# Chunk attention by blocks: small matmuls in place of masked full products

## The chip, the cores and the metric

The kernel runs on one NeuronCore of one Trainium2 chip. The metric is the device time of one execution in microseconds; the time before is the median of three runs. Engines are named as in the profile: PE is the matmul engine (PEld its weight loads), DVE is VectorE, ACT is ScalarE, POOL is GpSimd, SP is SyncE, which issues most transfers.

## The reference

One layer of an encoder, applied with the same weights to a sequence of 256 tokens and one of 512 (768 rows together, 1024 wide, all fp32): three mixers side by side, an output projection, and an MLP of width 4096. The change is in the first mixer, gated linear attention (GLA) in both directions, with 4 heads of 64 key and 128 value channels:

```python
def gla_scan(q, k, v, logg):
    ...
    def step(state, inp):
        qi, ki, vi, gi = inp
        b = jnp.cumsum(gi, axis=1)
        diff = b[:, :, None] - b[:, None, :]
        decay = jnp.exp(jnp.where(mask[:, :, None, None], diff, -jnp.inf))
        attn = jnp.einsum('bihd,bjhd,bijhd->bijh', qi, ki, decay)
        o = (jnp.einsum('bijh,bjhe->bihe', attn, vi)
             + jnp.einsum('bihd,bhde->bihe', qi * jnp.exp(b), state))
    ...
    logg_f = (jax.nn.log_sigmoid((r_f @ wg_f + bg_f).astype(jnp.float32)) / GLA_GATE_NORM
    ...
    o = gla_scan(q, k, v, logg_f) + flip(gla_scan(flip(q), flip(k), flip(v), flip(logg_b)))
    o = rmsnorm(o.astype(gv.dtype), norm_g)
    o = o * jax.nn.silu(gg.reshape(b_, s, GLA_HEADS, GLA_DV))
```

The decay is one for each key channel, so the attention within a chunk is not one product of q and k with a matrix over it. The other two mixers (differential attention, and a state-space mixer `ssd` whose `ssd_dt` is touched too) and the MLP follow the usual formulas.

## The kernel before

All 768 rows are kept as 6 tiles of 128 tokens (`NT`, two of the first sequence, four of the second). Large products split each fp32 operand in a rounded high part and a rest and add three products (`mm3`, lines 97 to 99); weights come in units over SP's queue (`load_unit`), are split by ACT (line 133) and DVE (line 134), and are consumed by `tm_unit` (tokens on the output partitions) or `fm_unit` (features on them).

The GLA mixer works on chunks of 128 tokens and on head pairs: the 64 key channels of two heads lie on 128 partitions, tokens on the free axis. There are two head pairs, one after the other. `gla_gates` makes the prefix sums of the log gates within each chunk, `Pf` forward and `Pb` backward, by a scan on DVE, in a layout of 129 columns for each chunk, column 0 being zero, so that both the inclusive sum (columns 1 to 128) and the exclusive one (0 to 127) can be read. `gla_core` then makes the chunk states `S` and the scaled queries `qst`, and the attention within each chunk by a binary splitting of the 128 tokens. At level s (64, 32, 16, 8, 4, 2, 1) tokens of the left half of each block of 2s meet those of the right half; the decay is taken relative to the boundary between the halves, so it splits in a factor for the query and one for the key. For each level DVE forms four differences of half the columns (lines 417, 418, 423, 424), ACT takes the exponentials (419, 425), DVE multiplies by q (420) and POOL by k (426). Then PE multiplies the whole 128x128 product for each chunk and head (435), and DVE copies from it into the attention tile `A`, by a mask, the elements that belong to this level (436). The diagonal is made apart: q times k summed over channels by PE (394, the tile `dps`, copied to `dg`), applied when the output `gout` is read (451). Lines 446 and 447 make the output, from `A` and from the states.

No order is written out by hand: the tile framework has a scheduler that fixes each engine's order from estimates of its own, and the engines then run in that order, waiting on semaphores. So the projections of other parts of the kernel (`tm`, `fm`) stand between the attention levels on PE where the scheduler put them. Scratch buffers come from pools of fixed numbers (`t3`, `c4`, `s3`, `t2`), and the results of small PE work from five banks of PSUM (`mx`).

Of the kernel before, what the change touches and what calls it, by code (L numbers as in the profile page):

```python
# [19 lines left out]
P = 128  # L20
# [7 lines left out]
N_IN, N_S3, N_T3, N_T2, N_TT, N_CC, N_DL, N_RAW, N_ACC = 12, 6, 6, 4, 8, 5, 7, 2, 3  # L28
# [3 lines left out]
W129 = NT * 129  # L32
# [10 lines left out]
def hybrid_kernel(ctx, tc, io):  # L43
# [31 lines left out]
    s3 = tag(first, "s3", N_S3, 776)  # L75

# [15 lines left out]
    def bc(ap, shape):  # L92
        return ap.to_broadcast(shape)
# [153 lines left out]
    resetm = s3("resetm", n=W129)  # L247
    pool.memset(resetm, 1.0)
    pool.memset(resetm.rearrange("p (c w) -> p c w", w=129)[:, :, 0:1], 0.0)

    def v129(t):
        return t.rearrange("p (c w) -> p c w", w=129)
# [11 lines left out]
    def gla_gates(hp):  # L264
        c0 = hp * P
        pre = []
        for d, r in ((0, R_BF), (1, R_BB)):
            bias = col(r + hp)
            rngs = ((0, 512), (512, 256))
            zs = [mx("gate"), mx("gate")]  # L270
            t1, g = t3("gt1"), t3("gt2", n=W129)
            v2 = v129(g)
            pool.memset(v2[:, :, 0:1], 0.0)
# [7 lines left out]
            dve.tensor_tensor(v2[:, :, 1:129], v2[:, :, 1:129], v128(t1), ALU.subtract)  # L281
            pf = s3("pre", n=W129)
            prefix(pf, g)
            pre.append(v129(pf))
        return pre
# [40 lines left out]

    def gla_core(pre, qk, v):
        Pf, Pb = pre
# [4 lines left out]
        kst = [t3("kst") for _ in range(2)]  # L333
        ef, eb = t3("ef"), t3("eb")
        act.activation(v128(ef), Pf[:, :, 1:129], AF.Exp, scale=0.0625)
        dve.tensor_tensor(v128(eb), bc(Pb[:, :, 128:129], [P, NT, P]), Pb[:, :, 0:128], ALU.subtract)
# [8 lines left out]
        dve.tensor_tensor(v128(kf), bc(Pf[:, :, 128:129], [P, NT, P]), Pf[:, :, 1:129], ALU.subtract)  # L345
        act.activation(kf, kf, AF.Exp, scale=0.0625)
        act.activation(v128(kb), Pb[:, :, 0:128], AF.Exp, scale=0.0625)
# [39 lines left out]
        A = [c4("A", n=T) for _ in range(2)]  # L387
        for a in A:
            pool.memset(a, 0.0)
        prod = t3("prod")  # L390
        pool.tensor_tensor(prod, q, k, ALU.mult)
        dps = mx("dps")
        for c in range(NT):
            mm(dps[:, 2 * c:2 * c + 2], lhsT=prod[:, c * P:(c + 1) * P], rhs=sel2, start=True, stop=True)
        dg = small("dg", 12).rearrange("p (c h) -> p c h", h=2)
        act.copy(dg, dps[:, :12].rearrange("p (c h) -> p c h", h=2))
        for li, s in enumerate(LEVELS):
            nb = P // (2 * s)

            def halves(ap, right):  # L400
                if nb == 1:
                    return ap[:, :, right * s:right * s + s]
                return ap.rearrange("p c (b r s) -> p c b r s", b=nb, r=2)[:, :, :, right, :]

            def inc(pp, right):
                return halves(pp[:, :, 1:129], right)

            def exc(pp, right):
                return halves(pp[:, :, 0:128], right)

            def ref(pp):
                if nb == 1:
                    return bc(pp[:, :, s:s + 1], [P, NT, s])
                return bc(exc(pp, 1)[:, :, :, 0:1], [P, NT, nb, s])

            eq = t3("eq")
            dve.tensor_tensor(halves(v128(eq), 1), inc(Pf, 1), ref(Pf), ALU.subtract)
            dve.tensor_tensor(halves(v128(eq), 0), ref(Pb), exc(Pb, 0), ALU.subtract)
            act.activation(eq, eq, AF.Exp, scale=0.0625)
            dve.tensor_tensor(eq, eq, q, ALU.mult)  # L420
            if s > 1:
                ek = t3("ek")
                dve.tensor_tensor(halves(v128(ek), 0), ref(Pf), inc(Pf, 0), ALU.subtract)
                dve.tensor_tensor(halves(v128(ek), 1), exc(Pb, 1), ref(Pb), ALU.subtract)
                act.activation(ek, ek, AF.Exp, scale=0.0625)
                pool.tensor_tensor(ek, ek, k, ALU.mult)
            else:
                ek = k
            for (a, b) in ((0, 4), (4, 6)):
                for h in range(2):  # L430
                    hs = slice(64 * h, 64 * h + 64)
                    ps = mx("att")
                    for c in range(a, b):
                        cs = slice(c * P, (c + 1) * P)
                        mm(ps[:, (c - a) * P:(c - a + 1) * P], lhsT=ek[hs, cs], rhs=eq[hs, cs], start=True, stop=True)
                    dve.copy_predicated(v128(A[h])[:, a:b, :], bc(masks[:, li, None, :], [P, b - a, P]),
                                        v128(ps[:, :(b - a) * P]))
# [3 lines left out]
        for h in range(2):  # L441
            for (a, b) in ((0, 4), (4, 6)):
                ps = mx("gout")
                for c in range(a, b):
                    o = (c - a) * P
                    mm(ps[:, o:o + P], lhsT=v128(A[h])[:, c, :], rhs=v128(v[h])[:, c, :], start=True, stop=False)
                    mm(ps[:, o:o + P], lhsT=qst[h][:, c * P:(c + 1) * P], rhs=S[h][:, c, :], start=False, stop=True)
                for c in range(a, b):
                    o = (c - a) * P
                    ov = v128(o_sb[h])[:, c, :]  # L450
                    dve.scalar_tensor_tensor(ov, v128(v[h])[:, c, :], dg[:, c, h:h + 1], ps[:, o:o + P],
                                             op0=ALU.mult, op1=ALU.add)
                    act.activation(junk[:, :P], ov, AF.Square, accum_out=ss[:, h, c:c + 1])
# [23 lines left out]
    def ssd_dt():  # L477
# [14 lines left out]
        dtl = t3("dtl", n=W129)  # L492
        lv_ = v129(dtl[ps_])
        pool.memset(lv_[:, :, 0:1], 0.0)

        dve.tensor_scalar(lv_[:, :, 1:129], v128(stk[0:16]), sdtc[0:16, 3:4], -128.0, op0=ALU.mult, op1=ALU.max)
        pre = t3("dpre", n=W129)
        pr = v129(pre)[ps_]
        dve.tensor_tensor_scan(pre[ps_], resetm[ps_], dtl[ps_], 0.0, ALU.mult, ALU.add)
        act.copy(v128(stk[32:48]), pr[:, :, 1:129])  # L500
        act.copy(v128(stk[64:80]), pr[:, :, 0:128])
        tot = bc(pr[:, :, 128:129], [16, NT, P])
        dve.tensor_tensor(v128(stk[96:112]), tot, pr[:, :, 1:129], ALU.subtract)
        stb = t3("stb")
        dve.tensor_tensor(v128(stb[0:16]), tot, pr[:, :, 0:128], ALU.subtract)
# [3 lines left out]
        nc.sync.dma_start(out=scr[0:8, :].rearrange("h (c i) -> h c i", i=P), in_=pr[0:8, :, 1:129])  # L509
        nc.sync.dma_start(out=scr[8:16, :].rearrange("h (c i) -> h c i", i=P), in_=pr[8:16, :, 0:128])  # L510
        nc.sync.dma_start(out=scp, in_=pr[:, :, 128])
# [485 lines left out]
    def col(r):  # L997
        return cols[:, r:r + 1]

    half = const.tile([P, 42], F32, name="half")  # L1000
# [10 lines left out]
    masks = t2("masks").bitcast(U8)[:, :len(LEVELS) * P].rearrange("p (l i) -> p l i", i=P)  # L1011
    for a, b in ((0, 4), (4, 7)):
        mraw = t2("mraw", n=(b - a) * P).rearrange("p (l i) -> p l i", i=P)
        nc.sync.dma_start(out=mraw, in_=io["c_masks"][:, a:b, :])
        pool.tensor_copy(masks[:, a:b], mraw)
# [4 lines left out]
    sel2 = const.tile([P, 2], F32, name="sel2")  # L1020
    pool.memset(sel2, 0.0)
    pool.memset(sel2[0:64, 0:1], 2.0)
    pool.memset(sel2[64:128, 1:2], 2.0)
# [145 lines left out]
def _constants():  # L1169
    i = np.arange(P)  # L1170
    masks = np.zeros((P, len(LEVELS), P), np.float32)
    for n, s in enumerate(LEVELS):
        masks[:, n, :] = (i[:, None] // (2 * s) == i[None, :] // (2 * s)) & (i[:, None] // s != i[None, :] // s)
# [28 lines left out]
```

## Time and profile before

| what | value |
|---|---|
| time, median of 3 runs | 1186.19 us (1180.62 to 1189.1) |
| the profiled execution | 1190.88 us, span 1188.8 us, mean granted clock 0.978 |
| PE busy | 1136.2 us (96%) |
| PE weight loads | 999.4 us (84%) |
| DVE busy | 768.7 us (65%) |
| ACT busy | 541.1 us (46%) |
| POOL busy | 162.8 us (14%) |
| first and last attention matmul of the levels (L435) | 120.1 and 237.8 us |

Busy is the time in which an engine had at least one instruction in work. PE's matmuls overlap (one starts before the last ends), so PE's busy time says that there was work, not how fast it went; the starts of neighbouring matmuls say that. "Idle before" is the time in which the engine had nothing in work just ahead of instructions of a group, with what ended it. The granted clock is PE's; 1.00 is full speed.

### The profile page before, as it was taken

To read this page: it belongs to the slowest core of one execution; us is meant where nothing else is said; L and a number is where in the kernel's file an instruction comes from. 1 tells how busy PE (TensorE), PEld (TensorE's weight loads), DVE (VectorE), ACT (ScalarE), POOL (GpSimd) and SP (SyncE) were. 2 spreads that over 40 slices of the span, in tenths; PEclk is the share of its full clock that TensorE was granted. 3 is DMA by queue.
4 is the path that set the end of the run, shared out by engine and by line. 5 is a ranking of instruction groups with operands and counts; after the bars stand their busy time and mean duration, and the time that the engine had idled before them with its cause. 6 is when DMAs were issued, how large, how long until landed. Compare 5 with 4: busy or idle time off the path is not lost.

```text
span 1188.8 us, 17623 instructions
## 1 busy us (share of the span) xinstructions
PE 1136.2 (96%) x6788; PEld 999.4 (84%) x6788; DVE 768.7 (65%) x1366; ACT 541.1 (46%) x1037; POOL 162.8 (14%) x207
## 2 busy tenths in 40 slices
PE   7979999999999998899988999999999999999998
PEld 7979899899998887698878897787987788787786
DVE  6558979775479577896786687766544444444443
ACT  7455345256266426665765673435322322322331
POOL 2003324140310262110100002200000000000000
PEclk9989999799999999899999999999999999999999
DMA  6312021143254346245645457642232232232331
GB/s 193 96 39 69 4 63 37 36 155 119 65 172 113 109 149 203 74 142 185 186 131 171 134 164 236 228 150 72 72 106 92 86 106 87 91 107 79 99 106 71
DMA packets 118856, 136.62 MB, mean 115 GB/s; under 512 B 8951, under 2 KB 86901, under 8 KB 118773
## 3 DMA queue, kind: packets, MB, share of 16 engines
q1 hardware_dynamic: 118741, 135.50, 36.7%
q8 instruction: 53, 0.87, 0.3%
q14 instruction: 30, 0.25, 0.1%
q10 hardware_dynamic: 32, 0.01, 0.0%
HBM read 121.80 MB, written 13.68 MB: 114 GB/s over the span
## 4 chain that ended last, share of the span: by engine, by line
PE 41%; DMA 12%; DVE 9%; ACT 6%; issue 2%; POOL 0%; SPq 0%; ACTq 0%; DVEq 0%; POOLq 0%
DMA wr<-in_w_mlp 8%; PE tp L97 7%; PE tp L98 7%; PE tp L99 7%; PE fm L97 5%; PE fm L98 5%; PE fm L99 5%; DVE wl L134 3%; ACT wh L133 3%; DMA wr<-in_w_out 2%; DMA er<-scr 1%; DVE zh L558 1%; DVE xres L877 1%; PE tm L97 1%; PE tm L99 1%
## 5 line engine op out<-in xcount | busy, mean ns | idle before, releaser
L133 ACT CAST wh<-wr 128x1024 fp32r<-128x1024 f32 x186 | 189.2, 1048 | 250.5 <-PE tp L99 128.2
L134 DVE TENSOR_TENSOR wl<-wr,wh 128x1024 fp32r<-128x1024 f32 x186 | 228.8, 1252 | 107.7 <-ACT wh L133 105.8
L99 PE MATMUL tm<-wh,hTl 128*128 128x256 f32 x576 | 169.8, 295 | 0.0
L97 PE MATMUL tm<-wh,hTh 128*128 128x256 f32 x576 | 168.0, 292 | 1.7 <-ACT xp L552 1.6
L98 PE MATMUL tm<-wl,hTh 128*128 128x256 f32 x576 | 168.2, 292 | 0.0
L877 DVE TENSOR_TENSOR xres<-tp,xres 128x512 f32<-128x512 f32 x116 | 77.7, 686 | 98.3 <-PE tp L99 98.0
L97 PEld LDWEIGHTS tm<-wh,hTh 128*128 128x128 f32 x576 | 112.3, 195 | 4.0 <-ACT xp L552 1.8
L98 PEld LDWEIGHTS tm<-wl,hTh 128*128 128x128 f32 x576 | 112.1, 195 | 1.7 <-DVE wl L134 0.2
L99 PEld LDWEIGHTS tm<-wh,hTl 128*128 128x128 f32 x576 | 112.2, 195 | 1.3
L98 PE MATMUL fm<-h2l,wh 128*128 128x512 f32 (+1 forms) x288 | 107.1, 373 | 0.0
L97 PE MATMUL fm<-h2h,wh 128*128 128x512 f32 (+1 forms) x288 | 106.9, 373 | 0.0
L99 PE MATMUL fm<-h2h,wl 128*128 128x512 f32 (+1 forms) x288 | 106.7, 371 | 0.0
L97 PE MATMUL tp<-wh,uh 128*128 128x512 f32 x256 | 101.5, 396 | 0.6
L98 PE MATMUL tp<-wl,uh 128*128 128x512 f32 x256 | 100.5, 392 | 0.0
L99 PE MATMUL tp<-wh,ul 128*128 128x512 f32 x256 | 99.7, 395 | 0.0
L97 PE MATMUL fm<-h,wh 128*128 128x256 f32 x256 | 72.3, 284 | 2.4 <-ACT relu L923 2.1
L98 PE MATMUL fm<-h,wh 128*128 128x256 f32 x256 | 72.2, 283 | 0.0
L99 PE MATMUL fm<-h,wl 128*128 128x256 f32 x256 | 71.5, 283 | 0.6 <-DVE wl L134 0.6
L923 ACT ACTIVATE relu<-fm 128x256 f32<-128x256 f32 (+1 forms) x68 | 31.6, 468 | 70.3 <-PE fm L99 70.3
L97 PEld LDWEIGHTS fm<-h2h,wh 128*128 128x128 f32 x288 | 54.7, 190 | 10.1
L99 PEld LDWEIGHTS fm<-h2h,wl 128*128 128x128 f32 x288 | 54.6, 190 | 10.0
L98 PEld LDWEIGHTS fm<-h2l,wh 128*128 128x128 f32 x288 | 54.7, 190 | 9.9
(323 smaller groups left out, 2499.4 us busy)
## 6 DMA issues: line engine op xcount, KB each, us to landing
wr<-in_w_mlp SPq DMA_DIRECT2D x128, 512.0 KB
wr<-in_w_in SPq DMA_DIRECT2D x30, 512.0 KB
wr<-in_w_out SPq DMA_DIRECT2D x24, 512.0 KB
ar<-scr SPq DMA_DIRECT2D x6, 512.0 KB
er<-scr SPq DMA_DIRECT2D x6, 512.0 KB
x<-in_x_sample SPq DMA_DIRECT2D x4, 512.0 KB
wr<-in_w_in SPq DMA_DIRECT2D x8, 256.0 KB
xres<-in_x_sample SPq DMA_DIRECT2D x4, 512.0 KB
```

What stands on the lines that cost most here:

```text
L97: mm(out, lhsT=lh, rhs=rh, start=first, stop=False)
L98: mm(out, lhsT=lh, rhs=rl, start=False, stop=False)
L99: mm(out, lhsT=ll, rhs=rh, start=False, stop=last)
L133: act.copy(hi, raw)
L134: dve.tensor_tensor(lo, raw, rd(hi), ALU.subtract)
L558: dve.scalar_tensor_tensor(zh, xp[:, k:k + 772], half[:, 6 * k + j:6 * k + j + 1], zh, op0=ALU.mult, op1=ALU.add)
L877: dve.tensor_tensor(xres[t][:, cs], ps, xres[t][:, cs], ALU.add)
L923: act.activation(r, ps, AF.Relu)
```

## The change

The attention of each level is no longer made as whole 128x128 products.

- At level 64 PE makes only the two 64x64 blocks off the diagonal for each chunk and head, at level 32 the four 32x32 blocks beside the diagonal, and ACT copies them to their places in `A`. No mask is used.
- At the levels 16 to 1 PE makes the four 32x32 blocks on the diagonal for each chunk and head, and DVE copies by a mask, of 32 columns, into a small tile `L` (two heads x 6 chunks x 32 columns). The diagonal is one more such product (of 2q and k) with its own mask. At the end ACT copies `L` into the diagonal blocks of `A`. The matmuls write to output partitions that start at 0, 32, 64 or 96 (0 or 64 for the large blocks). The tiles `dps`, `dg` and `prod` go, and the output is copied from PSUM by ACT in place of DVE's multiply and add.
- The prefix sums lie in 128 columns for each chunk. They are kept with the other sign, `Xf` inclusive, `Xb` exclusive with a separate total `tot`; for that the gates take `Relu` on ACT in place of add and min on DVE.
- The differences of a level are made whole: one DVE operation over all 768 columns for each direction, into a tile `d` of 2 x 768, in place of two of half the columns each. The exponentials and products are then made of halves: two of 384 columns for each one of 768.
- `ssd_dt` uses the 128-wide layout too, with one more DVE operation (`exc`), and the pool `t3` has 4 buffers in place of 6.

```diff
@@ gla_gates
             for z, (o, n) in zip(zs, rngs):
                 act.activation(t1[:, o:o + n], z[:, :n], AF.Abs, bias=bias)
-                dve.tensor_scalar(v2[:, o // P:(o + n) // P, 1:129], v128(z[:, :n]), bias, 0.0, op0=ALU.add, op1=ALU.min)
+                act.activation(g[:, o:o + n], z[:, :n], AF.Relu, bias=nbias, scale=-1.0)
...
@@ gla_core
+    def into_local(L, ps, i):
+
+        dve.copy_predicated(L, bc(masks[:, i, None, :], [P, NT, 32]), ps)
...
-        A = [c4("A", n=T) for _ in range(2)]
-        for a in A:
-            pool.memset(a, 0.0)
-        prod = t3("prod")
-        pool.tensor_tensor(prod, q, k, ALU.mult)
-        dps = mx("dps")
-        for c in range(NT):
-            mm(dps[:, 2 * c:2 * c + 2], lhsT=prod[:, c * P:(c + 1) * P], rhs=sel2, start=True, stop=True)
...
+        A = [v128(c4("A", n=T)) for _ in range(2)]
+        L = t2("L", n=12 * 32).rearrange("p (h c i) -> p h c i", h=2, c=NT)
+        pool.memset(L, 0.0)
+        k3 = v128(k)
+
+        def blocks(ps, h, w, left, right, across):
+
+            hs = slice(64 * h, 64 * h + 64)
+            for c in range(NT):
+                for b in range(P // w):
+                    o = b ^ across
+                    mm(ps[w * b:w * b + w, c, :], lhsT=left[hs, c, w * b:w * b + w], rhs=right[hs, c, w * o:w * o + w],
+                       start=True, stop=True)
+
         for li, s in enumerate(LEVELS):
...
-            dve.tensor_tensor(halves(v128(eq), 1), inc(Pf, 1), ref(Pf), ALU.subtract)
-            dve.tensor_tensor(halves(v128(eq), 0), ref(Pb), exc(Pb, 0), ALU.subtract)
-            act.activation(eq, eq, AF.Exp, scale=0.0625)
-            dve.tensor_tensor(eq, eq, q, ALU.mult)
+            for i, X in enumerate((Xb, Xf)):
+                x = parts(X)
+                ref = x[:, :, 1, 0:1] if i == 0 else x[:, :, 0, s - 1:s]
+                dve.tensor_tensor(D[i].rearrange("p b r i -> p b (r i)"), X.rearrange("p (b i) -> p b i", i=2 * s),
+                                  bc(ref, [P, nb, 2 * s]), ALU.subtract)
+            eq = t3("eq")
+            for i in range(2):
+                act.activation(D[i][:, :, i], D[i][:, :, i], AF.Exp, scale=-0.0625)
+                dve.tensor_tensor(parts(eq)[:, :, i], D[i][:, :, i], parts(q)[:, :, i], ALU.mult)
...
-            for (a, b) in ((0, 4), (4, 6)):
+            left, right = v128(ek), v128(eq)
+            if s == 64:
                 for h in range(2):
-                    hs = slice(64 * h, 64 * h + 64)
-                    ps = mx("att")
-                    for c in range(a, b):
-                        cs = slice(c * P, (c + 1) * P)
-                        mm(ps[:, (c - a) * P:(c - a + 1) * P], lhsT=ek[hs, cs], rhs=eq[hs, cs], start=True, stop=True)
-                    dve.copy_predicated(v128(A[h])[:, a:b, :], bc(masks[:, li, None, :], [P, b - a, P]),
-                                        v128(ps[:, :(b - a) * P]))
+                    ps = mx("att")[:, :NT * 64].rearrange("p (c i) -> p c i", c=NT)
+                    blocks(ps, h, 64, left, right, 1)
+                    act.copy(A[h][0:64, :, 64:128], ps[0:64])
+                    act.copy(A[h][64:128, :, 0:64], ps[64:128])
+                continue
+            for h in range(2):
+                ps = mx("att")[:, :NT * 32].rearrange("p (c i) -> p c i", c=NT)
+                blocks(ps, h, 32, left, right, int(s == 32))
+                if s < 32:
+                    into_local(L[:, h], ps, LOCAL.index(s))
+                    continue
+                for b in range(4):
+                    o = 32 * (b ^ 1)
+                    act.copy(A[h][32 * b:32 * b + 32, :, o:o + 32], ps[32 * b:32 * b + 32])
+
+        q2 = t3("q2")
+        act.activation(q2, q, AF.Copy, scale=2.0)
+        for h in range(2):
+            ps = mx("att")[:, :NT * 32].rearrange("p (c i) -> p c i", c=NT)
+            blocks(ps, h, 32, k3, v128(q2), 0)
+            into_local(L[:, h], ps, LOCAL.index(0))
+            for b in range(4):
+                act.copy(A[h][32 * b:32 * b + 32, :, 32 * b:32 * b + 32], L[32 * b:32 * b + 32, h])
...
-                    dve.scalar_tensor_tensor(ov, v128(v[h])[:, c, :], dg[:, c, h:h + 1], ps[:, o:o + P],
-                                             op0=ALU.mult, op1=ALU.add)
+                act.copy(o_sb[h][:, a * P:b * P], ps[:, :(b - a) * P])
```

How the order of instructions changes is seen best on PE, in the levels of the first head pair. Here `att` is the PSUM tile of a level's product for one head (numbers tell tiles apart), `tm` a projection between. Before, at the levels 16 and 8:

```order
L97 MATMUL tm_1653<-wh_1590,hTh_134 128x256
L435 MATMUL att_1117<-eq_1101,ek_1106 128x128 x4
L435 MATMUL att_1123<-eq_1101,ek_1106 128x128 x2
L98 MATMUL tm_1653<-wl_1591,hTh_134 128x256
L99 MATMUL tm_1653<-wh_1590,hTl_135 128x256
L97 MATMUL tm_1706<-wh_1590,hTh_120 128x256
L98 MATMUL tm_1706<-wl_1591,hTh_120 128x256
L435 MATMUL att_1127<-eq_1101,ek_1106 128x128 x2
L435 MATMUL att_1141<-eq_1131,ek_1136 128x128 x4
L99 MATMUL tm_1706<-wh_1590,hTl_121 128x256
```

After, at the end of the levels (level 2, level 1, and the diagonal from `q2`):

```order
L99 MATMUL tm_1981<-wl_1866,hTh_129 128x256
L412 MATMUL att_1355<-eq_1345,ek_1350 32x32 x24
L412 MATMUL att_1381<-eq_1345,ek_1350 32x32 x24
L412 MATMUL att_1415<-eq_1410,gk_821 32x32 x24
L412 MATMUL att_1441<-eq_1410,gk_821 32x32 x24
L412 MATMUL att_1469<-q_204_1467,gk_821 32x32 x24
L412 MATMUL att_1499<-q_204_1467,gk_821 32x32 x24
L100 MATMUL tm_1981<-wh_1865,hTl_130 128x256
```

The attention stands in fewer and longer runs: 26 runs of 2 to 16 matmuls before, 12 runs of 1 to 144 after, with projections between. Of the 425 matmuls from the first to the last of the first head pair's levels 360 are attention after the change, of 192 before 84.

On DVE, at the same stage. Before (`eq` and `ek` are the query and key factors of a level, `A` the attention tile, `pre` the prefix sums, `S` the states, `gg` the output gate):

```order
L436 COPY_PREDICATED A_1027<-masks_777,att_1067 128x256
L417 TENSOR_TENSOR eq_1131<-pre_727 128x48x8
L381 SCALAR_TENSOR_TENSOR S_1005<-S_1005,dec_935,U_1013 64x128
L418 TENSOR_TENSOR eq_1131<-pre_743 128x48x8
L423 TENSOR_TENSOR ek_1136<-pre_727 128x48x8
L424 TENSOR_TENSOR ek_1136<-pre_743 128x48x8
L436 COPY_PREDICATED A_1026<-masks_777,att_1081 128x512
```

After (`d` is a whole difference, `L` the small tile):

```order
L428 TENSOR_TENSOR d_1407<-pre_731 128x768
L338 COPY_PREDICATED L_1031<-masks_787,att_1251 128x192
L433 TENSOR_TENSOR eq_1345<-d_1342,gq_820 128x192x2 x2
L330 SCALAR_TENSOR_TENSOR gg_1864<-gg_1864,tm_1928 128x256
L338 COPY_PREDICATED L_1031<-masks_787,att_1290 128x192
L338 COPY_PREDICATED L_1031<-masks_787,att_1316 128x192
L433 TENSOR_TENSOR eq_1410<-d_1407,gq_820 128x384 x2
L428 TENSOR_TENSOR d_2167<-pre_780 128x768
L428 TENSOR_TENSOR d_2167<-pre_765 128x768
```

Two differences for a level stand where there were four, the masked copies are shorter, and the differences of the second head pair (`d_2167`) follow before the first one's levels are done.

More of the change, by code (lines that the diff above doesn't have):

```diff
@@ L75, in hybrid_kernel @@
     s3 = tag(first, "s3", N_S3, 776)
+    d2 = tag(first, "d2", 2, 2 * T)
     def small(name, n):
@@ new lines, in gla_core, with parts @@
+        for li, s in enumerate(LEVELS):
+            nb = T // (2 * s)
+            d = d2("d")
+            def parts(t):
+                return t.rearrange("p (b r i) -> p b r i", r=2, i=s)
+            D = [parts(d[:, i * T:(i + 1) * T]) for i in range(2)]
+            for i, X in enumerate((Xb, Xf)):
[3 more added lines that the diff above has]
+                                  bc(ref, [P, nb, 2 * s]), ALU.subtract)
@@ L421, in gla_core @@
             if s > 1:
                 ek = t3("ek")
[L423 to L426, printed above, removed]
+                for i in range(2):
+                    act.activation(D[1 - i][:, :, i], D[1 - i][:, :, i], AF.Exp, scale=0.0625)
+                    pool.tensor_tensor(parts(ek)[:, :, i], D[1 - i][:, :, i], parts(k)[:, :, i], ALU.mult)
@@ L491, in ssd_dt @@
         dve.scalar_tensor_tensor(stk[0:16], z, 0.0, l, op0=ALU.max, op1=ALU.add)
[L492 to L503, printed above, removed]
+        dtl = t3("dtl")[ps_]
+        dve.tensor_scalar(dtl, stk[0:16], sdtc[0:16, 3:4], -128.0, op0=ALU.mult, op1=ALU.max)
+        inc, exc = t3("dpre")[ps_], t3("dexc")[ps_]
+        dve.tensor_tensor_scan(inc, resetm[ps_], dtl, 0.0, ALU.mult, ALU.add)
+        dve.tensor_tensor(exc, inc, dtl, ALU.subtract)
+        act.copy(stk[32:48], inc)
+        act.copy(stk[64:80], exc)
+        tot = bc(v128(inc)[:, :, 127:128], [16, NT, P])
+        dve.tensor_tensor(v128(stk[96:112]), tot, v128(inc), ALU.subtract)
         stb = t3("stb")
-        dve.tensor_tensor(v128(stb[0:16]), tot, pr[:, :, 0:128], ALU.subtract)
+        dve.tensor_tensor(v128(stb[0:16]), tot, v128(exc), ALU.subtract)
         scr = dram.tile([16, T], F32, name="scr")
         scp = dram.tile([16, NT], F32, name="scp")
-        nc.sync.dma_start(out=scr[0:8, :].rearrange("h (c i) -> h c i", i=P), in_=pr[0:8, :, 1:129])
-        nc.sync.dma_start(out=scr[8:16, :].rearrange("h (c i) -> h c i", i=P), in_=pr[8:16, :, 0:128])
-        nc.sync.dma_start(out=scp, in_=pr[:, :, 128])
+        nc.sync.dma_start(out=scr[0:8, :], in_=inc[0:8])
+        nc.sync.dma_start(out=scr[8:16, :], in_=exc[8:16])
+        nc.sync.dma_start(out=scp, in_=v128(inc)[:, :, 127])
         ptb = const.tile([P, 2, 8, NT], F32, name="ptb")
@@ L998, in col @@
         return cols[:, r:r + 1]
+    nbf = const.tile([P, 4], F32, name="nbf")
+    dve.tensor_scalar(nbf, cols[:, R_BF:R_BF + 4], -1.0, None, op0=ALU.mult)
     half = const.tile([P, 42], F32, name="half")
@@ L1009, in hybrid_kernel @@
     pre = [gla_gates(hp) for hp in range(2)]
[L1011 to L1015, printed above, removed]
+    masks = t2("masks").bitcast(U8)[:, :len(LOCAL) * 32].rearrange("p (l i) -> p l i", i=32)
+    mraw = t2("mraw", n=len(LOCAL) * 32).rearrange("p (l i) -> p l i", i=32)
+    nc.sync.dma_start(out=mraw, in_=io["c_masks"])
+    pool.tensor_copy(masks, mraw)
     tri = const.tile([P, 2, P], F32, name="tri")
@@ L1019, in hybrid_kernel @@
     nc.sync.dma_start(out=rope, in_=io["c_rope"])
[L1020 to L1023, printed above, removed]
     qk16 = small("qk16", 32).rearrange("p (a d) -> p a d", a=2)
```

74 lines of the change are left out of this document (32 added, 42 removed).

## The prediction

> **What bounds the kernel now.** First the page's busy times and its row of slices, which say whether an engine is full and when.
>
> ```profile
> PE 1136.2 (96%) x6788; PEld 999.4 (84%) x6788; DVE 768.7 (65%) x1366; ACT 541.1 (46%) x1037; POOL 162.8 (14%) x207
> PE   7979999999999998899988999999999999999998
> DVE  6558979775479577896786687766544444444443
> PEclk9989999799999999899999999999999999999999
> ```
>
> TensorE (PE) is full nearly all the time and VectorE (DVE) is not, except where the change is made: digits 5 to 9, that is 120 to 270 us. The windows there are next; after the times come PE, weight loads, DVE, ACT and POOL busy, each with its count, then the granted clock.
>
> ```profile
> core 0: us, PE busy (x) PEld busy (x) DVE busy (x) ACT busy (x) POOL busy (x), PEclk, DMA share, GB/s
> 120.00:150.00 30.00, 28.37 (x228) 25.26 (x227) 29.75 (x51) 10.33 (x15) 9.30 (x5) 0.94 0.00 1
> 150.00:180.00 30.00, 30.00 (x256) 29.24 (x256) 22.50 (x50) 13.85 (x40) 7.71 (x15) 1.00 0.20 62
> 180.00:210.00 30.00, 27.96 (x241) 26.58 (x241) 27.69 (x42) 16.02 (x30) 13.32 (x6) 1.00 0.12 36
> 210.00:240.00 30.00, 30.00 (x186) 27.07 (x186) 22.23 (x37) 5.44 (x7) 4.25 (x2) 0.72 0.13 36
> ```
>
> In the first of these DVE has 29.75 of 30 us, so the attention levels go at DVE's pace; but PE is at 28.37, because the scheduler put projection matmuls (`tm`) between the levels. In the second PE has no hole at all, weight loads fill 29.24 us, and 256 matmuls run; the last window has only 186, at clock 0.72. The answer: in this stage PE is the resource that ends last, DVE is close behind, and an edit counts mainly by the PE time that it takes.
>
> **The attention matmuls, removed and added.** The rows by shape (line, engine, operation, tile, count, total us, mean ns, then idle before):
>
> ```profile
> L435 PE MATMUL att<-eq,ek 64*128 64x128 f32 x288 | 36.0, 301 | 3.7 <-DVE A L436 2.4 <-DVE S L381 1.3
> L435 PE MATMUL att<-eq,gk 64*128 64x128 f32 x48 | 5.3, 287 | 0.0
> 60.00:250.00 190.00, 40.57 (x336) 34.79 (x336) 29.66 (x56) 0.92 0.15 44
> L394 PE MATMUL dps<-sel,prod 128*128 128x2 f32 x24 | 2.8, 244 | 0.0
> L531 PE MATMUL tmb<-ident,stb 16*128 16x16 f32 x6 | 0.5, 211 | 0.0
> L629 PE MATMUL U<-wx,btm 128*64 128x256 f32 x32 | 4.1, 389 | 0.0
> ```
>
> The third row is the window of the `att` tiles alone, with overlaps counted once; the last two give the length of other small matmuls, for use below. The program writes 7 levels x 2 heads x 6 chunks x 2 head pairs = 168 matmuls; the trace has 336, so each fp32 matmul is two instructions, each with its weight load. I call such an instruction with its load a pair. Removed: 40.6 us of `att` and 2.8 us of `dps`, 43.4 us.
>
> Added: per head pair 24 blocks of 64x64, and 48 blocks of 32x32 for each of the six lower levels and for the diagonal (336): 360 matmuls. For both head pairs 720, hence 1440 pairs, over four times as many, each with a quarter of the columns or half. All hangs on the price of a small pair. Five places of the trace bear on it:
>
> ```profile
> 156.88 0.39 PE L446 MATMUL gout<-gv,A 128*128 128x128 f32 x2
> 162.01 0.39 PE L447 MATMUL gout<-S,qst 128*128 128x128 f32 x2
> 113.15 1.29 PE L394 MATMUL dps<-sel,prod 128*128 128x2 f32 x11
> 64.52 0.54 PE L531 MATMUL tmb<-ident,stb 16*128 16x16 f32 x6
> 416.68 1.08 PE L629 MATMUL U<-wx,btm 128*64 128x256 f32 x8
> 145.27 0.38 PE L98 MATMUL tm<-wl,hTh 128*128 128x256 f32 x1
> 145.59 0.72 PE L435 MATMUL att<-eq,ek 64*128 64x128 f32 x8
> 146.24 0.39 PE L99 MATMUL tm<-wh,hTl 128*128 128x256 f32 x1
> 146.46 0.28 PE L97 MATMUL tm<-wh,hTh 128*128 128x256 f32 x1
> 146.58 0.28 PE L98 MATMUL tm<-wl,hTh 128*128 128x256 f32 x1
> ```
>
> The output products: 46 pairs lie between the starts 156.88 and 162.01, so 0.112 us a pair with 128 columns. The `dps` pairs have 2 columns: (1.29 - 0.24) / 10 = 0.105 us (the last one's own length taken off, from the rows above, here and in what follows). Fewer moving columns alone bought nothing. The small transposes `tmb`: (0.54 - 0.21) / 5 = 0.066 us. Then overlap: `U` writes two halves of the output partitions in turn with 64 weight columns each, and takes (1.08 - 0.39) / 7 = 0.099 us a pair of 256 columns, half of what two streams of 128 columns would take: two parts of the array work at once. The same holds for the `att` row, where two heads lie on two halves of the contraction rows: (0.72 - 0.30) / 7 = 0.06 us.
>
> The new blocks write four strips of 32 partitions in turn, so overlap is to be expected, but no place shows more than two parts at once. I take a pair at half of 0.112, 0.056 us; it is also next to the 0.060 and 0.066 that were measured. Ends: 0.028 (four parts at once, an estimate from 0.112 / 4) and 0.112 (no gain from size, as with `dps`). So 1440 x 0.056 = 80.6 us; ends 40.3 and 161.3. Net on PE: 80.6 - 43.4 = +37.2 us, which lies on the path since PE has no hole to put it in.
>
> By the Trainium skill (TensorE: Matmul & The Clock Gate, the part on "56ns, not 53.3ns") starts never come closer than about 25 ns however few the columns, and where the sequencer decodes in software it spends about 62 ns a matmul; the first would make the added work 36 us and the net -7, the second 89 us and +46, and no run here shows which decoding is on. The skill's page TensorEngine Tiling (Array Packing), Instruction Overhead, speaks against the change: a matmul of one column takes as long as one of 60; the two columns of `dps` at 0.105 us agree that small does not mean cheap.
>
> **Entering and leaving.** From the `tm` at 145.27 to the `att` run is 0.32 us where 0.12 is usual: each run of `att` costs some 0.1 us to enter and 0.1 to leave, the latter already within the 40.6. By the order of instructions there are 26 runs before and 12 after: -14 x 0.1 = -1.4 us.
>
> **VectorE and the others.**
>
> ```profile
> L436 DVE COPY_PREDICATED A<-masks,att 128x512 f32<-128x512 uint8 x28 | 19.5, 727 | 6.9 <-PE att L435 6.8
> L436 DVE COPY_PREDICATED A<-masks,att 128x256 f32<-128x256 uint8 x28 | 11.2, 433 | 0.3
> L420 DVE TENSOR_TENSOR eq<-eq,gq 128x768 f32<-128x768 f32 x14 | 18.9, 1353 | 0.0
> L417 DVE TENSOR_TENSOR eq<-pre 128x384 f32<-128x384 f32 x14 | 9.4, 669 | 0.0
> L418 DVE TENSOR_TENSOR eq<-pre 128x384 f32<-128x384 f32 x14 | 9.3, 664 | 0.0
> L424 DVE TENSOR_TENSOR ek<-pre 128x384 f32<-128x384 f32 x12 | 8.2, 682 | 0.0
> L423 DVE TENSOR_TENSOR ek<-pre 128x384 f32<-128x384 f32 x12 | 7.7, 642 | 0.0
> L419 ACT ACTIVATE eq<-eq 128x768 f32<-128x768 f32 x14 | 11.9, 847 | 29.0 <-DVE eq L418 28.9
> L425 ACT ACTIVATE ek<-ek 128x768 f32<-128x768 f32 x12 | 10.1, 844 | 4.8 <-DVE ek L424 4.4
> 148.18 0.94 DVE L420 TENSOR_TENSOR eq<-eq,gq 128x768 f32<-128x768 f32 x1
> L293 ACT COPY gv<-tm 128x256 f32<-128x256 f32 x12 | 4.0, 374 | 10.4 <-PE tm L99 10.3
> ```
>
> DVE now spends 19.5 + 11.2 + 18.9 + 9.4 + 9.3 + 8.2 + 7.7 = 84.2 us on the levels. After: 28 whole differences of 768 at 0.94 (26.3 us), 28 half products at 0.67 (18.8, the upper price of a half row), 24 masked copies of 192, each 0.36 by the line through 727 and 433 ns (8.6): 53.7 us, 30 us less. ScalarE gets 52 half exponentials for 26 whole ones (each between half of 0.847 and the 0.67 of DVE's halves): 22.0 becomes 22 to 35 us, plus 40 block copies of 192 or 384 elements, near the 0.374 of the copy of 256: 15 us. POOL's products are only cut in two. The scheduler can hide all of this under PE's +37 us: DVE then needs 27 us a head pair for levels during which PE has 40 us of blocks. What DVE gives back is worth only what PE lost by waiting for it: the 3.7 us of idle before `att` above, and the clock. The 210 to 240 window lost 30 x 0.28 = 8.4 us to its 0.72; there PE waited between short runs. I take half of it back, 4.2 us, since blocks that use a quarter of the array may hold the clock down too; ends 0 and 8.4.
>
> The gates' DVE operations become ScalarE ones, the products `gv x dg` become copies, and the 129-wide layout goes: each is beside a full PE and costs nothing as long as PE stays behind; if PE were fast, ScalarE's added 15 to 28 us would show. The small wait of SyncE's queue before the gates (a store less ahead of `scp`) I leave at 0, ends -1 and +1. The scheduler also moves the later stages a little: 0, ends -5 and +5.
>
> **Sum.** +37.2 - 1.4 - 3.7 - 4.2 = +27.9 us. The profiled execution took 1190.9 us (span 1188.8), so 1218.8 in its terms; the median of the three runs is 4.7 lower, 1186.2, and gives **1214 us**.
>
> **Rivals.** *Four strips at once* (the other side). If a pair costs 0.028, PE's added work is 40.3 us and the sum is 40.3 - 43.4 - 1.4 - 3.7 - 4.2 = -12.4: 1174 us; with the whole clock back 1170. Less is not to be had, since DVE's 27 us a head pair then ends last, against 20 us of blocks. The overlap in `U` and in `att` speaks for it; that no row has a pair below 0.056 in a steady stream speaks against. It decides below 0.036 us, where the sum is 0. By the Trainium skill's 25 ns floor (same page as above) this is what would come: -17 us by its figure.
>
> *No overlap worth the name*: pairs at 0.085 to 0.112, as with `dps` and `gout`. 1440 x 0.085 = 122.4 gives +70, 1256 us; at 0.112 +109, 1295 us. For it: the strips follow each other so that each strip's two pairs are neighbours, and a pair of one strip must wait for the other. Against: `U` does the same and overlaps.
>
> *It cancels*: pairs at 0.036 to 0.045 us, sum 0 to +12, 1186 to 1198 us: the large change moves the work from DVE to PE with no visible gain.
>
> **Chances and range.** A change of under 1% (12 us) can't be told from none here, the three runs lying 8 us apart. Pairs of 0.045 to 0.075 us (the forecast, 1198 to 1242): 0.43. No overlap, above 0.075: 0.16. Cancelled or within 12 us either way (0.028 to 0.045): 0.23. Faster by more, pairs at 0.028 or below, with the clock back: 0.18. So slower 0.59, same 0.23, faster 0.18. The range of 8 in 10 leaves out the last part of the fast case and the worst of the slow one: 1173 to 1258. The likeliest sign's own range is 1198 to 1258.
>
> **What would show it.** The `att` rows: 1440 pairs, and the starts in a run of 24 matmuls (48 pairs): 2.7 us a run by the forecast, 1.3 by the fast rival, 5.4 by the slow one. PE's idle before `att` near 0 and DVE no longer above 9 tenths between 120 and 240 us; DVE's total near 740. The forecast is wrong if the `att` window holds under 55 us of PE, or if PE waits for DVE or ScalarE between levels, which would mean that the blocks are cheap and the chain of differences, exponentials and products has become the bound.

## The result and the profile after

The changed kernel takes **1169.4 us** (median of 4 runs, 1167.3 to 1172.1; the kernel before, on the same chip, 1187.6). The ratio is 0.987, with a 95% interval of 0.984 to 0.989: faster by about 1.3%, where 1214 us and a loss were forecast. The profiled execution took 1169.0 us (span 1167.2).

The page's busy times and three rows of its slices:

```profile
PE 1110.8 (95%) x7868; PEld 978.6 (84%) x7868; DVE 737.8 (63%) x1298; ACT 563.9 (48%) x1119; POOL 157.0 (13%) x208
PE   7989797999998999899989999999999999999998
DVE  6559859563697668887677786846544534434443
PEclk9989798899999999899999999999999999999999
```

PE has 1080 instructions more and is busy 25 us less. The 1440 small pairs are there (7868 - 6788 = 1080 is 1440 added, 336 and 24 removed). The digits of PE show where it now has holes: 7 in the fifth slice, 7 in the seventh, and the clock falls in the same places.

The levels, in two windows for each kernel that run from the first `att` matmul of a head pair to the last (times, then PE, weight loads, DVE, ACT and POOL busy with counts, clock). Before:

```profile
120.00:156.00 36.00, 34.37 (x278) 30.61 (x277) 35.75 (x61) 10.72 (x16) 9.30 (x5) 0.95 0.09 24
196.00:238.00 42.00, 39.96 (x270) 35.79 (x270) 34.90 (x56) 11.46 (x15) 9.39 (x5) 0.80 0.10 26
```

After, and below them the window of the `att` tiles alone:

```profile
114.00:143.00 29.00, 21.53 (x788) 19.69 (x786) 27.24 (x44) 18.68 (x46) 16.41 (x10) 0.80 0.01 4
185.00:213.00 28.00, 19.22 (x783) 18.06 (x784) 26.66 (x40) 18.20 (x41) 15.71 (x14) 0.82 0.08 20
60.00:250.00 190.00, 20.46 (x1440) 18.31 (x1440) 7.96 (x24) 8.70 (x24) 0.90 0.21 65
```

The levels of the two head pairs last 29 and 28 us in place of 36 and 42, 21 us less together, about as much as the span lost (1188.8 - 1167.2 = 21.6). The two are not the same 21 us: within the levels PE did 210 projection matmuls before and 126 after, and the other 84, some 10 us at 0.12 us each, now come later; on the other hand the levels begin 6 us earlier (at 114.1 in place of 120.1 us). DVE is busy for 27.24 of 29 us; PE, full before, has work in seven tenths of the time. The blocks take 20.46 us of PE, not 80.6.

How fast blocks go, and who keeps PE waiting, by the timeline of PE and the groups by shape:

```profile
118.42 1.02 PE L412 MATMUL att<-eq,ek 64*32 64x32 f32 x92
121.97 1.45 PE L412 MATMUL att<-eq,ek 64*32 64x32 f32 x96 [2.54 <-POOL ek L438]
128.77 1.05 PE L412 MATMUL att<-eq,ek 64*32 64x32 f32 x96
L412 PE MATMUL att<-eq,ek 64*32 64x32 f32 x960 | 12.5, 209 | 11.8 <-DVE eq L433 8.5 <-POOL ek L438 3.2
L428 DVE TENSOR_TENSOR d<-pre 128x768 f32<-128x768 f32 x28 | 31.9, 1181 | 1.6 <-POOL ek L438 1.5
L433 DVE TENSOR_TENSOR eq<-d,gq 128x384 f32<-128x384 f32 x28 | 20.5, 772 | 0.1
L338 DVE COPY_PREDICATED L<-masks,att 128x192 f32<-128x192 uint8 x24 | 8.0, 368 | 0.7 <-PE att L412 0.6
L438 POOL TENSOR_TENSOR ek<-d,gk 128x384 f32<-128x384 f32 x24 | 34.7, 1465 | 37.9 <-PE U L381 21.2 <-ACT d L437 6.0 <-DVE L L338 4.5
```

A run of 92 pairs takes 1.02 us: (1.02 - 0.209) / 91 = 0.009 us a pair. PE stands still for 11.8 us before blocks of the levels, 8.5 of it for DVE's products by q and 3.2 for POOL's by k. DVE itself hardly waits (0.1 to 1.6 us a group). So in the levels DVE, with POOL beside it, ends last.

Where the freed PE time went follows from the stretch from the start of the span to the start of the 1401st projection matmul (`tm`, `fm`, `tp`), added up from the trace, in us. Clock loss is time multiplied by one less the granted clock, idle time included, so that these two columns overlap; "rest" is what remains.

| | stretch | PE idle | clock loss | `att` | rest |
|---|---|---|---|---|---|
| before | 290.2 | 19.3 | 15.4 | 40.6 | 214.9 |
| after | 275.1 | 28.2 | 18.8 | 20.5 | 207.6 |
| after, strip by strip (below) | 276.2 | 15.0 | 6.8 | 40.3 | 214.1 |

Of the 20.1 us that `att` lost, 8.9 came back as idle time and 3.4 as clock. Another 6.4 us were gained from there to the end of the last matmul (894.7 to 888.3); a second profile of the changed kernel has 892.1 for that part, which leaves 2.6.

### The profile page after: what moved, and what is told of

Read it like the earlier page. It is cut to its first block, busy times and chain, and to the rows that moved or that the text cites. A ratio compares the mean times of both kernels' runs of the same rounds, so it can differ in the third digit from the quotient of the medians.

```text
span 1167.2 us, 19741 instructions
## 1 busy us (share of the span) xinstructions
PE 1110.8 (95%) x7868; PEld 978.6 (84%) x7868; DVE 737.8 (63%) x1298; ACT 563.9 (48%) x1119; POOL 157.0 (13%) x208
## 3 DMA queue, kind: packets, MB, share of 16 engines
q8 instruction: 62, 1.02, 0.3%
## 4 chain that ended last, share of the span: by engine, by line
PE 61%; DVE 16%; DMA 11%; ACT 6%; issue 3%; POOL 2%; SPq 0%; DVEq 0%; ACTq 0%; POOLq 0%
PE tp L98 7%; DMA wr<-in_w_mlp 7%; PE tp L99 7%; PE tp L100 7%; PE fm L98 6%; PE fm L100 6%; PE fm L99 6%; PE tm L100 5%; PE tm L99 5%; PE tm L98 5%; DVE wl L135 4%; ACT wh L134 2%; DMA er<-scr 1%; DVE d L428 1%; DVE eq L433 1%
## 5 line engine op out<-in xcount | busy, mean ns | idle before, releaser
L135 DVE TENSOR_TENSOR wl<-wr,wh 128x1024 fp32r<-128x1024 f32 x186 | 224.2, 1229 | 93.4 <-ACT wh L134 92.8
```

The costliest lines, as they stand in the source:

```text
L135: dve.tensor_tensor(lo, raw, rd(hi), ALU.subtract)
```

## The experiments

The theory formed from this trace (**Chain**): the differences, exponentials and products on DVE, ACT and POOL set the pace of the levels, and the blocks are so cheap that PE's time no longer counts there. Its rivals: PE's time still counts (**PE**), the gain comes from the differences made whole (**Whole**), or from the shorter chain of `ssd_dt` ahead of the gates (**Gates**). Ratios are to the kernel before, timed beside each run. After every edit the scheduler makes its order anew. Exchanging the loops changed the tile at 257 of the 7868 places in PE's order, doubling the masked copies at 994, moving POOL's products at 1206; so the levels themselves have to be read beside the time.

**Strips one after the other.** The changed kernel with the two loops of `blocks` exchanged, so that neighbouring matmuls write the same 32 partitions:

```diff
-            for c in range(NT):
-                for b in range(P // w):
+            for b in range(P // w):
+                for c in range(NT):
```

> The changed kernel with one loop order turned: the matmuls of a level go strip by strip (all six chunks of one strip of 32 output partitions, then the next strip) in place of the four strips in turn. Same matmuls, same data. Theory A, the small matmuls are cheap because four strips of the array work at once: neighbours now lie in the same strip and follow each other, so a pair rises from 0.009 us to between 0.03 and 0.06 us, attention takes 45 to 85 us of PE instead of 20, and the time goes to 1185 to 1215 us. Theory B, they are cheap because they are small: a pair stays near 0.009 us and the time at 1169 +- 4 us.

It takes 1168.95 us, ratio 0.984 (0.981 to 0.987). The windows of its levels, the window of its `att` tiles, a run on PE, and the group of the 32x32 blocks:

```profile
115.00:148.00 33.00, 31.10 (x792) 30.02 (x790) 28.08 (x45) 19.61 (x48) 16.06 (x10) 0.90 0.01 3
188.00:216.00 28.00, 27.76 (x785) 26.96 (x783) 25.65 (x38) 17.88 (x40) 15.30 (x14) 1.00 0.13 38
60.00:250.00 190.00, 40.26 (x1440) 38.92 (x1440) 8.35 (x24) 8.71 (x24) 0.96 0.20 63
118.56 2.41 PE L412 MATMUL att<-eq,ek 64*32 64x32 f32 x96
L412 PE MATMUL att<-eq,ek 64*32 64x32 f32 x960 | 26.2, 198 | 2.1 <-DVE eq L433 1.6 <-POOL ek L438 0.5
```

In one strip a pair takes (2.41 - 0.198) / 95 = 0.023 us in this run, in four strips in turn 0.009. So strips do overlap; and the 19.8 us that PE lost by it cost no time that could be measured. Neither expectation had both: the price rose, if less than the first said, and the time stayed as the second said. The table above shows what paid for the 19.8 us: 13.2 us less idle and 12.0 less clock loss, against 6.5 more of rest. The levels grew by 4 us, and PE is now the fuller engine there (58.9 of 61 us, DVE 53.7). So PE's time was free until PE's work in the levels had grown past DVE's. That is what Chain says of the changed kernel; by PE the time would have grown with the 19.8 us.

**DVE's work in the levels.** If Chain is right, work added on DVE must show where work added on PE did not:

```diff
-        dve.copy_predicated(L, bc(masks[:, i, None, :], [P, NT, 32]), ps)
+        for _ in range(2):
+            dve.copy_predicated(L, bc(masks[:, i, None, :], [P, NT, 32]), ps)
```

> The changed kernel with each of the 24 masked copies into the local tile done twice (the same values): 24 x 0.37 = 8.9 us more on VectorE inside the levels, nothing on PE. Theory Chain (VectorE with its neighbours ends last in the levels): the attention levels get 5 to 9 us longer and the time 3 to 9 us. Theory PE (PE ends last, as the prediction had it): VectorE's work lies beside PE and the time stays within 2 us of 1169.

1177.65 us, ratio 0.992 (0.990 to 0.995): 8.2 us more than the changed kernel, outside its interval. The same two windows, and the group that was doubled (its lines are one higher):

```profile
115.00:148.00 33.00, 25.00 (x791) 23.28 (x789) 30.72 (x53) 21.37 (x50) 15.81 (x10) 0.79 0.01 3
194.00:225.00 31.00, 22.20 (x789) 20.80 (x788) 28.62 (x48) 17.40 (x39) 19.06 (x14) 0.83 0.13 37
L339 DVE COPY_PREDICATED L<-masks,att 128x192 f32<-128x192 uint8 x48 | 15.2, 368 | 2.3 <-PE att L413 2.0
```

The levels grew from 29 and 28 to 33 and 31 us, the group by 7.2 us. DVE's work in the levels lengthens them about one for one, as Chain says. It does not follow that it costs the kernel as much, though the time grew by 8.2 us. PE did 169 projection matmuls in these longer levels, not 126, and in the two profiles the 1601st starts at the same moment (302.1 and 302.2 us; this one has 24 small matmuls of the differential attention still ahead of it). It falls behind in the next hundred projection matmuls, which last 26.0 us in place of 13.5, with PE idle for 6.7 us and a clock of 0.80. How much of that is DVE's added work, and how much the new order, is not shown.

**POOL's part in the chain.** The products by k go to DVE:

```diff
-                    pool.tensor_tensor(parts(ek)[:, :, i], D[1 - i][:, :, i], parts(k)[:, :, i], ALU.mult)
+                    dve.tensor_tensor(parts(ek)[:, :, i], D[1 - i][:, :, i], parts(k)[:, :, i], ALU.mult)
```

> The changed kernel with the products of k (line 438) on DVE instead of POOL. Theory A, in the levels PE now waits for the chain difference, exponential, product, in which POOL's 1.5 us a half and DVE's operations lengthened beside it (differences 1.18 us instead of 0.95) are the slow part: DVE gains 24 x 0.55 = 13 us of work and loses as much by running undisturbed, the chain is shorter, 1158 to 1166 us. Theory B, DVE's load is the bound in the levels: 13 us more on DVE cost 4 to 10 us, 1173 to 1180 us.

> The changed kernel with line 438's products on VectorE once more, in five rounds beside the changed kernel. Theory Chain: GpSimd's products (1.47 us each, and VectorE slowed beside them) are part of the chain, so 3 to 8 us faster than the changed kernel. Theory Total work: within 2 us of it.

> The changed kernel itself once more, beside the others of this call, as the measure for the small differences: 1167 to 1172 by every theory.

The first run gave 1166.65 us, ratio 0.982 (0.979 to 0.986). Run again it gave 1164.62, 0.981 (0.978 to 0.985), beside the changed kernel itself at 1168.70, 0.985 (0.982 to 0.989). So 3 to 4 us, twice in the same direction, though the intervals overlap. It is the fastest version that was run. Its groups (the first run):

```profile
L428 DVE TENSOR_TENSOR d<-pre 128x768 f32<-128x768 f32 x28 | 25.5, 950 | 0.0
L433 DVE TENSOR_TENSOR eq<-d,gq 128x384 f32<-128x384 f32 x28 | 14.9, 551 | 0.1
L438 DVE TENSOR_TENSOR ek<-d,gk 128x384 f32<-128x384 f32 x24 | 12.9, 551 | 0.1
```

DVE took over 24 products at 551 ns, 12.9 us, and its total did not change (738.2 against 737.8 us): the differences fell from 1181 to 950 ns and the products by q from 772 to 551, 12.0 us together. What POOL seemed to take off DVE it cost DVE in slower operations. The changed kernel itself shows this too: its 12 whole differences with no POOL work beside them take 949 ns on average, the 16 others 1355; its 15 half products without, 547 ns, the 13 others 1031. The masked copies take 367 to 371 either way. The Trainium skill (Perfetto Trace Analysis, Optimizing Scalar/DVE Operations) says that the two share a read port of the SBUF, so that moving work between them may not help; the traces agree as to DVE's total.

The levels did not get shorter by it (30 and 28 us, DVE busy for 54.5 us of them, 53.9 in the changed kernel). What changed is that PE does 250 projection matmuls in them in place of 126, some 15 us of work. The 3 to 8 us that were expected came, then, but not by a shorter chain. The stretch to the 1401st projection matmul is 14 us shorter (261.3), but the rest of the kernel 9 us longer (897.0), and likewise in the second run (257.8 and 902.2). Most of that is given back in one place, the same as with the doubled copies: the hundred projection matmuls from the 1601st on last 26.5 us in both runs and 13.5 in the changed kernel. PE is idle for 7.2 us there, 4.7 of it for ACT's `dv` and 2.5 for DVE's `ms`, both of the differential attention, and the clock is 0.81. The clock loss of the whole later part is 13.7 and 17.1 us, the changed kernel's 8.5 and, in its second profile, 10.2.

**Both edits.** Products on DVE and blocks strip by strip:

> The changed kernel with both edits that were tried singly: line 438's products on VectorE and the blocks written strip by strip, which made a pair take some 28 ns instead of 9 and so added 20 us of PE in the levels at no cost (1169.0). Theory Chain: with GpSimd out of the chain the levels are shorter, but VectorE still ends last (about 27 us a head pair against 20 us of blocks), so the 20 us of PE again cost under 4 us: 1165 to 1170. Theory PE near: the shorter chain has used up PE's slack and the blocks now show, 1173 to 1185.

1177.71 us, ratio 0.992 (0.989 to 0.995): 11 to 13 us slower than with the products on DVE alone. Its windows of the levels, and two groups:

```profile
115.00:154.00 39.00, 39.00 (x877) 37.90 (x875) 31.11 (x59) 21.61 (x50) 0.00 (x0) 1.00 0.11 30
197.00:229.00 32.00, 30.27 (x787) 29.44 (x787) 25.39 (x48) 17.28 (x38) 2.07 (x4) 0.92 0.14 36
L412 PE MATMUL att<-eq,ek 64*32 64x32 f32 x960 | 24.9, 194 | 0.0
L338 DVE COPY_PREDICATED L<-masks,att 128x192 f32<-128x192 uint8 x24 | 8.9, 371 | 13.6 <-PE att L412 13.5
```

Chain missed here. In the first head pair PE is full, its wait before the blocks is 0.0, and DVE waits 13.5 us for PE before its masked copies. The reason can be read from the two engines' busy time in the levels, both head pairs together, in us (the length is that of the windows):

| | length | PE busy | DVE busy | projection matmuls |
|---|---|---|---|---|
| before | 78 | 74.3 | 70.6 | 210 |
| after | 57 | 40.8 | 53.9 | 126 |
| strip by strip | 61 | 58.9 | 53.7 | 139 |
| masked copies twice | 64 | 47.2 | 59.3 | 169 |
| products on DVE | 58 | 50.9 | 54.5 | 250 |
| both edits | 71 | 69.3 | 56.5 | 236 |

In each row the levels last a little longer than the fuller engine is busy. With the products on DVE the scheduler had already put so many projections into the levels that PE had 7 us left; 20 us more could not fit, and 50.9 + 20 = 71 is about what the levels took. Chain holds for the changed kernel, not for what is made of it: PE and DVE are close, and the order decides which of them ends last.

**One part of the change alone.** The kernel before with only the blocks (129-wide layout and half differences kept), and with only the new `ssd_dt`:

> The kernel before with the blocks alone (small matmuls, small tile, masks of 32 columns, diagonal by a matmul, copies by ScalarE); the layout of 129 columns, the gates, the four half differences of a level and ssd_dt stay as before. Theory A, the gain is PE time given back by the blocks: att about 20 us of PE, 1170 to 1176 us. Theory B, the gain comes from the differences, the gates, the layout and a new schedule: 1182 to 1190 us, though att is just as short.

> The kernel before with ssd_dt alone changed (128 columns for a chunk, exclusive sums by one more DVE operation, the store of the chunk totals issued earlier); the attention is as before. If the 4 us by which the gates start earlier in the changed kernel come from this, and are kept to the end: 1182 to 1185 us, idle PE before the gates' matmuls 3 to 5 us instead of 7.5. If they are taken back by the full PE behind them, or come from elsewhere: 1186 to 1190 us.

The blocks alone: 1175.86 us, ratio 0.990 (0.988 to 0.993), about 11 us. `ssd_dt` alone: 1181.72 us, 0.995 (0.992 to 0.997), about 6 us, with no block in it, but with a changed order (127 projection matmuls in the first head pair's levels, 108 before). Then each part undone in the changed kernel, `ssd_dt` first, and after it the differences, made of halves:

```diff
-                dve.tensor_tensor(D[i].rearrange("p b r i -> p b (r i)"), X.rearrange("p (b i) -> p b i", i=2 * s),
-                                  bc(ref, [P, nb, 2 * s]), ALU.subtract)
+                for r in range(2) if s > 1 else (i,):
+                    dve.tensor_tensor(D[i][:, :, r], x[:, :, r], bc(ref, [P, nb, s]), ALU.subtract)
```

> The changed kernel with one part undone: the 129-wide layout of the discretisation chain (ssd_dt) comes back, the rest stays. Theory Two parts (blocks and the shorter chain ahead of the gates each save by themselves, 12 and 6 us, and add): about 6 us are lost, 1174 to 1177, and the last gate ends some 3 to 4 us later than the changed kernel's 79.8 us. Theory Overlap (the shorter chain's gain is swallowed once the levels are bound by VectorE): under 2 us are lost, 1169 to 1171.

> The changed kernel with one part undone: each level again subtracts only the halves that it uses (four half subtractions in place of two whole ones, two at the last level). Theory Chain (the levels go at the pace of the chain VectorE - ScalarE - GpSimd, PE is not the bound): what counts is VectorE's time in the levels; whole ones measured 1.18 us each, so 28 x 1.18 = 33 us against 52 halves of about 0.67 = 35 us; the time is within 4 us of the changed kernel's (1167 to 1174). Theory Whole (making the differences whole is where the gain comes from, half rows being dear): at least 6 us are lost again, 1175 or more.

With the old `ssd_dt` the time is 1167.67 us, 0.986 (0.982 to 0.991): no loss is seen, with some 5 us of scatter either way. With half differences it is 1173.49, 0.988 (0.984 to 0.993), 4 to 5 us more than the changed kernel, within the scatter. Half the columns in 672 ns, whole in 1181, come to the same DVE time (32.0 and 31.9 us):

```profile
L429 DVE TENSOR_TENSOR d<-pre 128x384 f32<-128x384 f32 x52 | 32.0, 672 | 1.6 <-POOL ek L438 1.5
```

So Whole falls as the main cause. Gates is half right at most: the new `ssd_dt` brings 6 us in the kernel before, by its shorter chain or by the new order, and nothing that could be measured in the changed one. By the ratios the blocks bring some 11 us of the 16 to 17 (0.987 and, run again, 0.985); the other 5 or 6 belong to no single part that was tried, and stay open.

**More projections between the blocks.** Since PE has holes in the levels, the output-gate projections of each head pair were written ahead of its levels (products on DVE as above; the first head pair's is shown), and in a second version only the first head pair's, ahead of the second's `gla_qk` and `gla_v`:

```diff
     qk = gla_qk(0)
+    sg = gla_gate_out(0)
     core = gla_core(pre[0], qk, v)
     qk, v = gla_qk(1), gla_v(1)
-    sg = gla_gate_out(0)
```

> The changed kernel with the products of line 438 on VectorE in place of GpSimd (as in the run that did this alone: 1166.7) and the output-gate projections of each head pair written ahead of its levels, so that the scheduler has more projection matmuls to put between the runs of blocks. Theory Chain: PE's idle time in 110 to 240 us and the drop of the granted clock that goes with it are filled by work that otherwise comes later, 5 to 12 us less, 1155 to 1162. Theory Total work (PE's work and clock set the end whatever the order): no difference, 1165 to 1168. A loss would mean that the gate's own ScalarE and VectorE work gets in the way of the levels.

> The changed kernel with the products of line 438 on VectorE, and the output-gate projections of the first head pair written between its levels and the query, key and value projections of the second (in the run that wrote them ahead of the levels PE stood still for 14 us behind VectorE's gg at line 330 in 90 to 120 us, and the time was 1177). Theory Chain with a full ring: without that stop the projections fill PE's holes between the runs of blocks, 1158 to 1164. Theory Total work: 1165 to 1169, as with the products on VectorE alone (1166.7).

1176.99 us (0.991, 0.989 to 0.994) and 1172.06 us (0.988, 0.984 to 0.991): neither gains. Both meet a new wait ahead of the levels. In the first:

```profile
102.83 0.66 PE L98 MATMUL fm<-hTh,wh 128*128 128x384 f32 x1 [14.15 <-DVE gg L330]
```

PE stands still for 14.15 us behind DVE's operation on the output gate (`gg`); in the second version it is 14.29 us behind the same line. The holes in the levels were not filled for free, and whether they can be is not shown.

## Why the prediction was wrong

**The price of a pair was the step that failed**: "I take a pair at half of 0.112, 0.056 us". It is 0.009 us in a run, and 20.46 / 1440 = 0.014 with the ends of the runs, a quarter of the price taken and half of its lower end. Two things were folded into one factor of two. The first is size: in a single strip a pair takes 0.023 us, not 0.112. The rows that seemed to say that small is not cheap did not have the blocks' shape: `dps` at 0.105 us had two moving columns, but 128 weight columns. It is these that count in the rows here: the median distance between neighbouring starts is 112 ns for `dps` (2 moving columns) and for `gout` (128) and 111 for the old `att` (64 rows), all with 128 weight columns; in the strip-by-strip kernel it is 58 ns for the blocks with 64 weight columns and 27 for those with 32. (The transposes `tmb`, of 16 rows, are the exception, 62 ns with 128.) The second is the overlap of the strips: a further 0.023 / 0.009 = 2.6, or 40.26 / 20.46 = 2.0 with the ends of the runs. The prediction had a trace of overlap in its evidence (`U`, `att`) and then settled in the middle of its bounds.

With the measured 20.5 us the sum reads 20.5 - 43.4 - 1.4 - 3.7 - 4.2 = -32.2 us, 1154. That is too low by 15, so a second step was wrong.

**"In this stage PE is the resource that ends last ... an edit counts mainly by the PE time that it takes"**: in the changed kernel it does not. 20 us of PE more lengthened the levels by 4 us and the time not at all, 7 us of DVE more lengthened the levels by 7. The rival "Four strips at once" had this: "Less is not to be had, since DVE's 27 us a head pair then ends last, against 20 us of blocks". The levels last 29 and 28 us with DVE busy for 27.24 and 26.66. And the strip-by-strip kernel is close to this rival in its terms too: 40.26 us of blocks where it assumed 40.3, PE nearly full in the levels, 4.3 us of idle time and 8.6 of clock back in the stretch above where it took 3.7 and at most 8.4, and 1169 us where it gave 1170 to 1174. Halving the blocks again moved nothing. What the prediction gave as the sign that it is wrong, under 55 us in the `att` window and PE waiting for DVE between levels, is what the trace has.

**The terms that follow from it.** The 3.7 us of waiting before `att` did not go but became 11.8. The 4.2 us of clock did not come back: the loss in the first stretch rose from 15.4 to 18.8 us. Both were taken as gains in a sum in which PE was full; with PE in waiting they have the other sign. (The reason given for the clock has a slip: a block has 64 of 128 rows and 32 of 128 columns, an eighth and not a quarter. So has the price of entering a run of `att`: the line quoted gives 0.32 - 0.12 = 0.2 us, not 0.1. Over the 21 places with a projection just ahead the median is 0.09, so the 1.4 us stand.)

**VectorE.** The total was right (near 740; 737.8), as was the masked copy (0.36; 0.368). But the levels took 31.9 + 20.5 + 8.0 = 60.4 us, not 53.7: a whole difference 1.18 us and not 0.94, a half product 0.772 and not 0.67. "POOL's products are only cut in two" missed it: in the shorter levels POOL works for 16.41 of 29 us and not 9.30 of 36, and DVE's operations stretch beside it. The 0.94 us came from a row at a moment when POOL stood still (its products ran from 143.42 for 1.83 us, the row at 148.18); with POOL out of the way the difference takes 0.950 us. The 6.7 us more lay in the levels, where DVE ends last.

**ScalarE and the gates.** ACT's added 22.8 us (541.1 to 563.9) lie in the 15 to 28 forecast. Leaving `ssd_dt` and the queue ahead of `scp` at 0 agrees with the changed kernel, where undoing it showed no loss; alone, in the kernel before, it came with 6 us. The wait of the first tile after it shrank by 2 us (by 1 in the second profile). Before, and after:

```profile
74.96 0.58 ACT L519 ACTIVATE decs<-ptb 64x48 f32<-64x48 f32 x2 [9.20 <-DMA ptb<-scp]
```

```profile
70.78 0.58 ACT L543 ACTIVATE decs<-ptb 64x48 f32<-64x48 f32 x2 [7.20 <-DMA ptb<-scp]
```

**The Trainium skill's figures.** The floor that the prediction quoted from the Trainium skill (TensorE: Matmul & The Clock Gate, the part on "56ns, not 53.3ns"), about 25 ns from start to start, would have given the right sign. The blocks in one strip are near it, at 23 to 27 ns; the run of 92 over four strips is well below it, at 9 ns, and there the measurement decides. The page of the Trainium skill that was read as speaking against the change, TensorEngine Tiling (Array Packing), also says under Key Properties that different tiles can load weights and multiply in parallel. That part is what the two loop orders show, 0.023 against 0.009 us.

## What to carry to other kernels

Price a small matmul by its whole shape, weight rows and columns as well as moving columns, and by the order in which neighbouring ones use the strips of the array; where bounds are 1 to 4 apart, work the time out at each end before choosing, since here the lower end had another engine as its bound. When two engines are both over nine tenths full in a stage, an edit that relieves both has to be priced by the one that is left with more: add up the second engine's work for the stage and compare. To find which one ends last, add a little work to one engine at a time and read the stage itself: 20 us on PE lengthened the levels by 4 us, 7 us on DVE by 7. Where a scheduler makes the order, compare the order as well before the time is put down to the edit: with the products moved to DVE the levels were as long as in the changed kernel, but held twice the projections.

## What the runs showed of the hardware

- The matmul instructions of fp32 blocks of 64 rows and 32 weight columns with 32 moving columns (two for each block, each with its weight load) start every 9 ns on average within a run when four strips of output partitions are written in turn, and every 23 to 27 ns in one strip.
- DVE's fp32 two-input operations run 24% and 40% longer (950 to 1181 ns, 551 to 772 ns) with POOL's products in the same levels than without, so that the products moved back to DVE for no more DVE time. In the changed kernel the operations with no POOL work beside them take 949 and 547 ns, and its masked copies are not slowed.
- The granted clock was 0.80 and 0.82 in the levels in which PE waits, and 1.00 and 0.92 where the same blocks kept it busy (strip by strip, with the products on DVE). But before the change it was 0.80 in the second window with PE busy for 39.96 of 42 us, so a busy PE alone does not keep it up.
